# Longer target transfers, earlier statistics and a recut tail in a normalised squared-error loss

## The chip, the cores and the metric

One core of a Trainium2 chip. The time is device microseconds of one execution; lower is better. The profiler's span is some 1.7 us shorter than the reported time (75.1 to 76.86 for the kernel before). Times inside an execution count from the start of that span.

## The reference, cut to what matters

```python
# pred, target: [32, 147, 768] float32
mean = target.mean(axis=-1, keepdims=True)
var = target.var(axis=-1, keepdims=True)
target = (target - mean) / np.sqrt(var + 1e-6)
loss = np.mean((pred - target) ** 2, axis=-1)
return loss.mean(axis=-1)                      # [32]
```

Each of 4704 rows of 768 is normalised by its own mean and variance and compared with its prediction. The 28.9 MB of input are read once; the output is 32 numbers.

## The kernel before

The rows are laid out as 36 columns of 128 rows, 0 to 35, and a rest of 96 rows. A column's way: target and pred are loaded by DMA (all but the first pieces cast to bf16 on the way, issued by GpSimd); VectorE makes the target's statistics; ScalarE takes the root; VectorE the reciprocal; GpSimd normalises into `s`. Then pred minus s is squared and summed in one of three ways: TensorE forms -s + pred in PSUM with two products by identity matrices and ScalarE squares it ("ACT"); VectorE subtracts and ScalarE squares ("DVE+ACT"); or VectorE does both ("DVE"). Below, the "subtraction of 34" is TensorE's product that puts -s of column 34 into PSUM, the "product of 34" the one that adds its pred, and "square 34" ScalarE's square of the result. Towards the end each column, or pair of columns, is split between the first and the last way. The order on each engine is worked out beforehand by a small scheduler from estimated durations, a rank and an earliest time for each operation.

```python
piece("p", 0, 4)
piece("t", 16, 20)          # four columns a transfer
piece("t", 20, 24)
piece("p", 4, 8)
piece("t", 24, 28)
piece("t", 28, 32)
piece("p", 8, 12)
piece("t", 32, 36)
# ... pred in fours to 23, twos to 31, ones to 34, and 35 in two halves
piece("p", KM - 1, KM, 0, half)
piece("p", KM - 1, KM, half, D)
# ...
units = [((c, c + 1), 0, D, "ACT" if c < 14 else "DVE+ACT") for c in range(0, 24, 2)]
# ...
for u in [(c, c + 1) for c in range(26, KM - 4, 2)] + [(c,) for c in range(KM - 4, KM - 1)]:
    m = BANK if u[0] < KM - 2 else half
    units += [(u, 0, m, "ACT"), (u, m, D, "DVE")]
units += [((KM - 1,), 0, half, "ACT"), ((KM - 1,), half, D, "DVE")]
# ... the tail's PSUM tiles, two banks each whatever they hold
pools["parts"] = ctx.enter_context(tc.tile_pool(name="parts", bufs=3, space=bass.MemoryType.PSUM))
zs[u, d0] = pools["parts"].tile([P, 2 * BANK], F32, name="zp")
```

KM is 36, D 768, half 384, BANK 512 (the fp32 columns of one PSUM bank).

Of the kernel before, what the change touches and what calls it, by code (L numbers as in the profile page):

```python
# [7 lines left out]
F32 = mybir.dt.float32  # L8
BF16 = mybir.dt.bfloat16
ALU = mybir.AluOpType  # L10
# [4 lines left out]
def kernel(  # L15
# [9 lines left out]
    B, N, D = pred.shape  # L25
    eps = 1e-6
    P = 128
    J = P // B
    KJ = (N + J - 1) // J
    KM = N - (J - 1) * KJ  # L30
    assert KJ == KM + 1
    RP = B * (J - 1)
    half = D // 2
    BANK = 512
    REST = KM
# [4 lines left out]
    def rows_of(c):  # L40
        return RP if c == REST else P
# [12 lines left out]
    def piece(kind, c0, c1, d0=0, d1=D, q="sw"):  # L54
        stream.append((kind, c0, c1, d0, d1, q))
# [5 lines left out]
    piece("p", REST, REST + 1)  # L61
    piece("t", 12, 16)
    piece("p", 0, 4)
    piece("t", 16, 20)
    piece("t", 20, 24)
    piece("p", 4, 8)
    piece("t", 24, 28)
    piece("t", 28, 32)
    piece("p", 8, 12)
    piece("t", 32, 36)  # L70
    for c in range(12, 24, 4):
# [2 lines left out]
        piece("p", c, c + 2)  # L74
    for c in range(32, 35):
        piece("p", c, c + 1)
    piece("p", KM - 1, KM, 0, half)
    piece("p", KM - 1, KM, half, D)


    groups = [(0, 1), (2, 3), (REST,)] + [tuple(range(c, c + 4)) for c in range(4, KM, 4)]


    units = [((c, c + 1), 0, D, "ACT" if c < 14 else "DVE+ACT") for c in range(0, 24, 2)]
    units.insert(2, ((REST,), 0, D, "ACT"))
    units += [((24,), 0, D, "DVE"), ((25,), 0, D, "DVE+ACT")]
    for u in [(c, c + 1) for c in range(26, KM - 4, 2)] + [(c,) for c in range(KM - 4, KM - 1)]:
        m = BANK if u[0] < KM - 2 else half
        units += [(u, 0, m, "ACT"), (u, m, D, "DVE")]
    units += [((KM - 1,), 0, half, "ACT"), ((KM - 1,), half, D, "DVE")]  # L90



# [3 lines left out]
    def op(name, engine, dur, needs, fn, rank=0.0, early=0.0):  # L97
        by_name[name] = len(ops)
        ops.append((name, engine, dur, needs, fn, rank, early))
# [17 lines left out]
    for i, (kind, c0, c1, d0, d1, q) in enumerate(stream):  # L117
        w = (c1 - c0) * (d1 - d0)
        clock += w * rows_of(c0) / P * 0.915 / D + (0.0 if w >= 4 * D else 0.04)
        lanes[q].append(clock + 1.1)  # L120
        for c in range(c0, c1):
            land[kind, c, d0] = clock + 1.1
        k = len(lanes[q])
        op(("load", i), {"hw": "SP", "hw2": "ACT", "sw": "POOL"}[q], 0.6, [], lambda a=stream[i]: load(*a), rank=-1.0,
           early=0.0 if k <= 8 else lanes[q][k - 9] + 0.3)

    def landed(kind, c):
        return max(t for (k, cc, d), t in land.items() if k == kind and cc == c)

    ident = singles.tile([P, P], BF16)  # L130
# [25 lines left out]
    def bn(out, parts):  # L156

        n = parts[0].shape[0]
        st = small.tile([P, len(parts), 6], F32, name="st")
        for j, x in enumerate(parts):  # L160
            pin(nc.vector.bn_stats(out=st[:n, j, :], in_=x))  # L161
        pin(nc.vector.bn_aggr(out=out, in_=st[:n, :len(parts)]))  # L162

    def stats(g, i):
        n, K = rows_of(g[0]), len(g)
        if i == 0:
            mvs[g] = small.tile([P, K, 2], F32, name="mv")
        if not norm_pix_loss:
            return
        (_, _, til, o), = tbuf[g[i]]  # L170
        bn(mvs[g][:n, i], [til[:n, o + a:o + a + half] for a in (0, half)])

    def root(g):
        n, K = rows_of(g[0]), len(g)
        r = small.tile([P, K], F32, name="r")
        nm = small.tile([P, K], F32, name="nm")
        for i, c in enumerate(g):
            rs[c] = (r[:n, i:i + 1], nm[:n, i:i + 1])
        rs[g] = r
        if not norm_pix_loss:  # L180
            pin(nc.vector.memset(r, 1.0))
            pin(nc.vector.memset(nm, 0.0))
            return
        mv = mvs[g]
        pin(nc.scalar.activation(out=r[:n], in_=mv[:n, :, 1], func=ACTF.Sqrt, bias=eps_t[:n], scale=1.0))  # L185
        pin(nc.scalar.activation(out=nm[:n], in_=mv[:n, :, 0], func=ACTF.Copy, scale=-1.0))  # L186

    def recip(g):
        n = rows_of(g[0])
        if norm_pix_loss:  # L190
            pin(nc.vector.reciprocal(out=rs[g][:n], in_=rs[g][:n]))  # L191

    for k, g in enumerate(groups):
        for i, c in enumerate(g):
            op(("bn", c), "DVE", 1.26, [], lambda g=g, i=i: stats(g, i), rank=k - 50.0 if c < 32 or c == REST else -1.5, early=landed("t", c))
        op(("root", k), "ACT", 0.55, [("bn", c) for c in g], lambda g=g: root(g), rank=-1.0)
        op(("recip", k), "DVE", 0.2, [("root", k)], lambda g=g: recip(g), rank=-60.0)

# [16 lines left out]
    zs = {}  # L215
# [5 lines left out]
    def product(u, d0, w, src, so, eye, first):  # L221
        n, z = rows_of(u[0]), zs[u, d0]

        runs = [(0, so, w)] if w % D == 0 else [(k * BANK, so + k * D, w // len(u)) for k in range(len(u))]
        for zo, o, e in runs:
            for a in range(0, e, BANK):
                b = min(e, a + BANK)
                pin(nc.tensor.matmul(z[:n, zo + a:zo + b], eye[:n, :n], src[:n, o + a:o + b],  # L228
                                     start=first, stop=not first))

    def sub_target(u, d0, w):
        if u in pairs_pe:
            zs[u, d0] = pools["pairs"].tile([P, 3 * BANK], F32, name="z")
            pairs_pe.remove(u)
        else:
            if "parts" not in pools:

                pools["stack"].close()
                pools["parts"] = ctx.enter_context(tc.tile_pool(name="parts", bufs=3, space=bass.MemoryType.PSUM))
            zs[u, d0] = pools["parts"].tile([P, 2 * BANK], F32, name="zp")  # L240
        s, so = sbuf[u[0]]
        product(u, d0, w, s, so + d0, nident, True)

# [30 lines left out]
    rl = singles.tile([P, n_early], F32)  # L274
    rl_sum = singles.tile([P, 1], F32)
    pairs_pe = [u for u, d0, d1, eng in units if eng == "ACT" and (u[0] == REST or len(u) * (d1 - d0) > 2 * BANK)]
    n_pairs = len(pairs_pe)
    pools = {"stack": ExitStack()}
    pools["pairs"] = pools["stack"].enter_context(tc.tile_pool(name="psum", bufs=2, space=bass.MemoryType.PSUM))
    finals = []  # L280
    early_ops, users, dusers, dprev, seen = [], [], [], [], set()
    for k, (u, d0, d1, eng) in enumerate(units):
        w = len(u) * (d1 - d0)
        arrive = max(t for (kk, c, d), t in land.items() if kk == "p" and c in u and d < d1)
        norms = [("norm", c) for c in u]
        for c in u:
            if c not in seen:
                op(("norm", c), "POOL", 1.02, [("recip", group_of[c])], lambda u=u, c=c: normalise(u, c), rank=k)
                seen.add(c)
        if k < len(units) - tail:  # L290
            if u[0] == REST:
                dest = singles.tile([P, 1], F32, name="rl_rest")
                finals.append((("sq", k), dest, mask_rest, RP))
            else:
                dest = rl[:, len(early_ops):len(early_ops) + 1]
                early_ops.append(("sq", k))
        else:
            dest = singles.tile([P, 1], F32, name=f"rl{k}")
            finals.append((("sq", k), dest, mask, P))
        if eng in ("DVE", "DVE+ACT"):  # L300
            op(("diff", k), "DVE", 0.57 * w / D + 0.05, norms + dusers[-5:-4] + dprev[-1:], lambda u=u, d0=d0, w=w: difference(u, d0, w), rank=-2.0,
               early=arrive)
            dusers.append(("sq", k))
            dprev.append(("diff", k))
            if eng == "DVE":
                op(("sq", k), "DVE", 1.0 * w / D, [("diff", k)],
                   lambda u=u, d0=d0, w=w, dest=dest: square_dve(u, d0, w, dest), rank=-1.0)
            else:
                op(("sq", k), "ACT", 0.65 * w / D + 0.22, [("diff", k)],
                   lambda u=u, d0=d0, w=w, dest=dest: square_act(u, d0, w, dest), rank=k)  # L310
            continue
        op(("subt", k), "PE", 0.37 * w / D, norms + (users[-2:-1] if len(users) < n_pairs else users[n_pairs - 1:n_pairs] + users[n_pairs:][-3:-2]) + ["ident"],
           lambda u=u, d0=d0, w=w: sub_target(u, d0, w), rank=k + 0.0)
        op(("pred", k), "PE", 0.37 * w / D, [("subt", k)], lambda u=u, d0=d0, w=w: add_pred(u, d0, w), rank=k,
           early=arrive)
        op(("sq", k), "ACT", 0.65 * w / D + 0.22, [("pred", k)],
           lambda u=u, d0=d0, w=w, dest=dest: square_act(u, d0, w, dest), rank=k)
        users.append(("sq", k))

    acc = psum1.tile([1, B], F32)  # L320
    op("rl_sum", "DVE", 0.2, early_ops, lambda: pin(nc.vector.tensor_reduce(
        out=rl_sum, in_=rl, axis=mybir.AxisListType.X, op=ALU.add)), rank=-3.0)
    finals.insert(0, ("rl_sum", rl_sum, mask, P))
    turn = []

# [5 lines left out]
    for i, (need, vec, m, n) in enumerate(finals):  # L331
        op(("final", i), "PE", 0.2, [need, "masks"], lambda v=vec, m=m, n=n: final(v, m, n), rank=90.0,
           early=max(land.values()) + 0.4)
# [6 lines left out]
    while left:  # L340
        best = None
        for i in left:
            name, engine, dur, needs, fn, rank, early = ops[i]
            if any(x not in end for x in needs):
                continue
            t = max([free[engine], early] + [end[x] + (0.0 if ops[by_name[x]][1] == engine else HOP) for x in needs])
# [4 lines left out]
        _, i, t = best  # L351
        name, engine, dur, needs, fn, rank, early = ops[i]
# [43 lines left out]
```

## Time and profile before

| | before |
|---|---|
| time, median of the first 3 runs | 76.86 us (76.75 to 76.93) |
| span | 75.1 us |
| busy share: PE, DVE, ACT, POOL | 39%, 75%, 40%, 71% |
| DMA share of the software queue | 89% |
| last landing (the last of its 16 completion records) | 71.59 us |
| end of the last sum | 72.65 us (VectorE) |

Read it from the DMA row: only the stream of transfers is busy throughout, so the time is the stream plus what has to follow the last landing. The second part is 72.65 - 71.59 = 1.06 us up to the last sum. The row for the clock that TensorE was granted, in tenths of full speed for 40 slices of 1.88 us:

```profile
PEclk9999999999999999999999755599555797555995
```

It falls to half in stretches, one of which ends at 69.6 us, just before the tail.

### The profile page before, as it was taken

What the parts mean: (1) busy time and instruction counts of PE and PEld (TensorE: products, weight loads), DVE (VectorE), ACT (ScalarE), POOL (GpSimd) and SP (SyncE); (2) the same over time, 40 slices, a digit from 0 to 9 for tenths busy, and PEclk for the clock granted to TensorE, in tenths of its full rate; (3) what the DMA queues carried; (4) which work ended last, traced back from release to release, by engine and by line L of the source; (5) the groups of instructions that cost most, each with busy time, mean ns of one, the idle gap of its engine ahead of it and who ended that gap; (6) DMA issues with size and microseconds to landing.
All of it is one profiled execution on the core that took longest, in us unless ns stands there. A gap on an engine that the chain in (4) does not pass through costs nothing.

```text
span 75.1 us, 551 instructions
## 1 busy us (share of the span) xinstructions
PE 29.0 (39%) x81; PEld 8.3 (11%) x82; DVE 56.3 (75%) x155; ACT 30.4 (40%) x65; POOL 53.7 (71%) x75
## 2 busy tenths in 40 slices
PE   0000000385004989405973006740709300379760
PEld 0000000011001233002121002110103000112130
DVE  0000399999999999999959999375797389998870
ACT  5100001400202696020690010890099969965950
POOL 6998103999499989398989898987695999900000
PEclk9999999999999999999999755599555797555995
DMA  0799999999999999999999999999999999999900
GB/s 0 196 425 317 234 265 218 193 226 213 219 222 209 219 217 209 209 216 213 209 226 219 220 209 219 209 209 213 213 209 232 196 212 214 213 204 208 148 0 0
DMA packets 3685, 15.41 MB, mean 205 GB/s; under 512 B 418, under 2 KB 1154, under 8 KB 3554
## 3 DMA queue, kind: packets, MB, share of 16 engines
q0 software_dynamic: 3424, 13.52, 89.0%
q1 hardware_dynamic: 258, 1.87, 6.9%
q14 instruction: 3, 0.02, 0.1%
HBM read 28.90 MB, written 0.00 MB: 385 GB/s over the span
## 4 chain that ended last, share of the span: by engine, by line
DMA 51%; POOL 32%; issue 7%; DVE 3%; ACT 2%; PE 2%; POOLq 0%
DMA p<-in_pred_dram 29%; POOL s L211 25%; DMA t<-in_target_dram 22%; POOL p L111 4%; ACT zp L249 2%; POOL t L111 2%; DVE zd L269 2%; PE zp L228 1%; DVE zd L265 1%; POOL ident L139 0%; POOL nident L139 0%; PE acc L328 0%; DVE ob L359 0%; POOL nident L138 0%; POOL ident L138 0%
## 5 line engine op out<-in xcount | busy, mean ns | idle before, releaser
L161 DVE BATCH_NORM_STATS2 st<-t 128x6 f32<-128x384 bf16 (+2 forms) x74 | 36.2, 530 | 10.4 <-DMA t<-in_target_dram 10.4
L211 POOL TENSOR_SCALAR s<-t,nm,r 128x768 bf16<-128x768 bf16 (+2 forms) x37 | 38.3, 1043 | 6.2 <-DVE r L191 5.5
L228 PE MATMUL z<-p,ident 128*128 128x512 bf16 (+2 forms) x23 | 10.4, 614 | 18.3 <-DMA p<-in_pred_dram 18.3
L228 PE MATMUL z<-s,nident 128*128 128x512 bf16 (+2 forms) x23 | 9.8, 546 | 16.2 <-POOL s L211 14.9
L249 ACT ACTIVATE z<-z 128x1536 f32<-128x1536 f32 (+1 forms) x8 | 10.9, 1357 | 11.6 <-PE z L228 11.6
L185 ACT ACTIVATE r<-mv,eps_t 128x4 f32<-128x4 f32 (+2 forms) x11 | 3.2, 292 | 27.4 <-DVE mv L162 26.6
L265 DVE TENSOR_TENSOR zd<-p,s 128x1536 bf16<-128x1536 bf16 (+4 forms) x14 | 9.6, 701 | 3.6 <-DMA p<-in_pred_dram 3.5
L111 POOL DMA_DIRECT2D p<-in_pred_dram x16 | 9.1, 570 | 3.5 <-DMA t<-in_target_dram 1.3
L162 DVE BATCH_NORM_AGGREGATE mv<-st 128x2 f32<-128x12 f32 (+1 forms) x37 | 7.7, 208 | 1.3
L249 ACT ACTIVATE zd<-zd 128x1536 bf16<-128x1536 bf16 (+1 forms) x6 | 8.2, 1364 | 0.7 <-DVE zd L265 0.7
L228 PEld LDWEIGHTS <-ident 128*128 128x128 bf16 (+1 forms) x33 | 4.4, 134 | 33.4 <-issue 33.1
L228 PE MATMUL zp<-p,ident 128*128 128x512 bf16 (+1 forms) x9 | 4.3, 519 | 6.9 <-DMA p<-in_pred_dram 6.9
L228 PEld LDWEIGHTS <-nident 128*128 128x128 bf16 (+1 forms) x33 | 3.5, 122 | 29.7 <-issue 16.6
L249 ACT ACTIVATE zp<-zp 128x1024 f32<-128x1024 f32 (+2 forms) x7 | 5.1, 735 | 1.5 <-PE zp L228 1.4
L111 POOL DMA_DIRECT2D t<-in_target_dram x8 | 4.7, 612 | 1.1 <-DMA t<-in_target_dram 1.1
L228 PE MATMUL zp<-s,nident 128*128 128x512 bf16 (+1 forms) x10 | 4.7, 571 | 2.1 <-ACT z L249 1.7
L269 DVE SCALAR_TENSOR_TENSOR zd<-zd 128x512 bf16<-128x512 bf16 (+3 forms) x8 | 5.0, 623 | 0.2
L186 ACT ACTIVATE nm<-mv 128x4 f32<-128x4 f32 (+2 forms) x11 | 2.1, 189 | 0.0
L185 ACT ACT_TABLE_LOAD x1 | 1.3, 1283 | 0.8 <-PEq L377 0.8
L249 ACT ACTIVATION_READ_ACCUMULATOR z<-z 128x1 f32 (+1 forms) x8 | 1.5, 190 | 0.0
L191 DVE RECIPROCAL r<-r 128x4 f32<-128x4 f32 (+2 forms) x11 | 1.4, 128 | 0.1
L249 ACT ACTIVATION_READ_ACCUMULATOR zp<-zp 128x1 f32 x7 | 1.3, 188 | 0.0
(25 smaller groups left out, 7.0 us busy)
## 6 DMA issues: line engine op xcount, KB each, us to landing
t<-in_target_dram POOLq DMA_DIRECT2D x8, 768.0 KB, 23.7
p<-in_pred_dram POOLq DMA_DIRECT2D x6, 768.0 KB, 29.0
t<-in_target_dram SPq DMA_DIRECT2D x1, 1536.0 KB, 8.0
p<-in_pred_dram POOLq DMA_DIRECT2D x4, 384.0 KB, 24.5
p<-in_pred_dram POOLq DMA_DIRECT2D x3, 192.0 KB, 16.4
t<-in_target_dram SPq DMA_DIRECT2D x1, 288.0 KB, 10.6
p<-in_pred_dram POOLq DMA_DIRECT2D x2, 96.0 KB, 9.5
p<-in_pred_dram POOLq DMA_DIRECT2D x1, 144.0 KB, 13.2
```

The costliest lines, as they stand in the source:

```text
L111: pin(eng.dma_start(out=til[:n], in_=src))
L161: pin(nc.vector.bn_stats(out=st[:n, j, :], in_=x))
L162: pin(nc.vector.bn_aggr(out=out, in_=st[:n, :len(parts)]))
L185: pin(nc.scalar.activation(out=r[:n], in_=mv[:n, :, 1], func=ACTF.Sqrt, bias=eps_t[:n], scale=1.0))
L186: pin(nc.scalar.activation(out=nm[:n], in_=mv[:n, :, 0], func=ACTF.Copy, scale=-1.0))
L191: pin(nc.vector.reciprocal(out=rs[g][:n], in_=rs[g][:n]))
L211: pin(nc.gpsimd.tensor_scalar(out=s[:n, so:so + D], in0=til[:n, o:o + D], scalar1=nm, scalar2=r, op0=ALU.add, op1=ALU.mult))
L228: pin(nc.tensor.matmul(z[:n, zo + a:zo + b], eye[:n, :n], src[:n, o + a:o + b], start=first, stop=not first))
L249: pin(nc.scalar.activation(out=z[:n, :w], in_=z[:n, :w], func=ACTF.Square, accum_out=dest[:n]))
L265: pin(nc.vector.tensor_tensor(out=x, in0=y, in1=v, op=ALU.subtract))
L269: pin(nc.vector.scalar_tensor_tensor(out=z, in0=z, scalar=1.0, in1=z, op0=ALU.mult, op1=ALU.mult, accum_out=dest))
```

## The change

Its intent: two transfers fewer; no subtraction of VectorE in front of a statistic, so that the last normalisations aren't late; one pair (14, 15) taken off VectorE; a last part with less for VectorE; and PSUM tiles of the size that is used, so that more of the tail's first products (by s) are made ahead of pred. The diff, comments and unchanged lines cut:

```diff
-    piece("t", 16, 20)
-    piece("t", 20, 24)
+    piece("t", 16, 24)
     piece("p", 4, 8)
-    piece("t", 24, 28)
-    piece("t", 28, 32)
+    piece("t", 24, 32)
 ...
-    piece("p", KM - 1, KM, 0, half)
-    piece("p", KM - 1, KM, half, D)
+    piece("p", KM - 1, KM, 0, BANK)
+    piece("p", KM - 1, KM, BANK, D)
 ...
-    units = [((c, c + 1), 0, D, "ACT" if c < 14 else "DVE+ACT") for c in range(0, 24, 2)]
+    units = [((c, c + 1), 0, D, "ACT" if c < 16 else "DVE+ACT") for c in range(0, 24, 2)]
 ...
-        m = BANK if u[0] < KM - 2 else half
-        units += [(u, 0, m, "ACT"), (u, m, D, "DVE")]
-    units += [((KM - 1,), 0, half, "ACT"), ((KM - 1,), half, D, "DVE")]
+        units += [(u, 0, BANK, "ACT"), (u, BANK, D, "DVE")]
+    units += [((KM - 1,), 0, BANK, "ACT"), ((KM - 1,), BANK, D, "DVE")]
 ...
-            op(("bn", c), ... rank=k - 50.0 if c < 32 or c == REST else -1.5, ...)
+            op(("bn", c), ... rank=k - 50.0 if c < 36 or c == REST else -1.5, ...)
 ...
-                pools["parts"] = ... bufs=3 ...
-            zs[u, d0] = pools["parts"].tile([P, 2 * BANK], F32, name="zp")
+                pools["parts"] = ... bufs=2 ...
+                pools["last"] = ... bufs=3 ...
+            if len(u) == 2:
+                zs[u, d0] = pools["parts"].tile([P, 2 * BANK], F32, name="zp")
+            else:
+                zs[u, d0] = pools["last"].tile([P, BANK], F32, name="zl")
 ...
-    op("rl_sum", ... rank=-3.0)
+    op("rl_sum", ... rank=3.0)
```

More of the change, by code (lines that the diff above doesn't have):

```diff
@@ L194 @@
         for i, c in enumerate(g):
-            op(("bn", c), "DVE", 1.26, [], lambda g=g, i=i: stats(g, i), rank=k - 50.0 if c < 32 or c == REST else -1.5, early=landed("t", c))
+            op(("bn", c), "DVE", 1.26, [], lambda g=g, i=i: stats(g, i), rank=k - 50.0 if c < 36 or c == REST else -1.5, early=landed("t", c))
         op(("root", k), "ACT", 0.55, [("bn", c) for c in g], lambda g=g: root(g), rank=-1.0)
@@ L238, in sub_target @@
                 pools["stack"].close()
-                pools["parts"] = ctx.enter_context(tc.tile_pool(name="parts", bufs=3, space=bass.MemoryType.PSUM))
-            zs[u, d0] = pools["parts"].tile([P, 2 * BANK], F32, name="zp")
+                pools["parts"] = ctx.enter_context(tc.tile_pool(name="parts", bufs=2, space=bass.MemoryType.PSUM))
+                pools["last"] = ctx.enter_context(tc.tile_pool(name="last", bufs=3, space=bass.MemoryType.PSUM))
+            if len(u) == 2:
+                zs[u, d0] = pools["parts"].tile([P, 2 * BANK], F32, name="zp")
+            else:
+                zs[u, d0] = pools["last"].tile([P, BANK], F32, name="zl")
         s, so = sbuf[u[0]]
@@ L280 @@
     finals = []
-    early_ops, users, dusers, dprev, seen = [], [], [], [], set()
+    early_ops, users, dusers, dprev, pusers, lusers, seen = [], [], [], [], [], [], set()
     for k, (u, d0, d1, eng) in enumerate(units):
@@ L311 @@
             continue
-        op(("subt", k), "PE", 0.37 * w / D, norms + (users[-2:-1] if len(users) < n_pairs else users[n_pairs - 1:n_pairs] + users[n_pairs:][-3:-2]) + ["ident"],
+        op(("subt", k), "PE", 0.37 * w / D, norms + (users[-2:-1] if len(users) < n_pairs else users[n_pairs - 1:n_pairs] + (pusers[-2:-1] if len(u) == 2 else lusers[-3:-2])) + ["ident"],
            lambda u=u, d0=d0, w=w: sub_target(u, d0, w), rank=k + 0.0)
@@ L318 @@
         users.append(("sq", k))
+        if len(users) > n_pairs:
+            (pusers if len(u) == 2 else lusers).append(("sq", k))
     acc = psum1.tile([1, B], F32)
     op("rl_sum", "DVE", 0.2, early_ops, lambda: pin(nc.vector.tensor_reduce(
-        out=rl_sum, in_=rl, axis=mybir.AxisListType.X, op=ALU.add)), rank=-3.0)
+        out=rl_sum, in_=rl, axis=mybir.AxisListType.X, op=ALU.add)), rank=3.0)
     finals.insert(0, ("rl_sum", rl_sum, mask, P))
```

## The prediction

> **What bounds the kernel now.** I read the page first, then the chain of waits in order of time, then the timelines of VectorE, TensorE and ScalarE from 49 us on. From the page, the rows for the share of the DMA engines and for what was read:
>
> ```profile
> span 75.1 us, 551 instructions
> ...
> DMA  0799999999999999999999999999999999999900
> ...
> HBM read 28.90 MB, written 0.00 MB: 385 GB/s over the span
> ```
>
> No slice from 3.8 us to 71 us is below nine tenths, while the same page gives VectorE 75% and GpSimd 71%. So the stream of transfers is the bound: 28.9 MB in about 68.5 us is 422 GB/s. The chain of waits names GpSimd for much of the way, but only because GpSimd issues each transfer after one eight places earlier has landed; what decides is its last part:
>
> ```profile
> 45.97 21.79 DMA p<-in_pred_dram
> 67.75 0.04 issue
> 67.79 1.03 PE zp L228 x2
> 68.82 0.02 issue
> 68.84 0.87 ACT zp L249
> 69.71 0.05 issue
> 69.76 0.80 ACT zp L249 x3
> 70.56 0.02 issue
> 70.59 0.05 DVE rl_sum L321
> ...
> 72.07 0.58 DVE zd L269 x2
> 72.65 0.04 issue
> 72.70 0.23 PE acc L328 x2
> 72.93 0.02 issue
> 72.95 0.18 DVE ob L359
> ```
>
> The transfer of pred 30 and 31 was issued at 45.97 and landed at 67.75, so eight queued transfers always hide the issue. After it come the tail's squares, VectorE's last difference and sum (end 72.65), one product (72.93), a copy, the store. From 72.65 to the end of the span is 2.47 us and from span to reported time 1.74 us; neither is touched.
>
> How long a piece occupies the stream is read from what ended waits:
>
> ```profile
> 49.35 1.02 DVE L161 BATCH_NORM_STATS2 st<-t 128x6 f32<-128x384 bf16 x2 [1.72 <-DMA t<-in_target_dram]
> 53.09 0.96 DVE L265 TENSOR_TENSOR zd<-p,s 128x1536 bf16<-128x1536 bf16 x1 [1.28 <-DMA p<-in_pred_dram]
> 56.74 0.96 DVE L265 TENSOR_TENSOR zd<-p,s 128x1536 bf16<-128x1536 bf16 x1 [0.40 <-DMA p<-in_pred_dram]
> 64.07 0.58 PE L228 MATMUL zp<-p,ident 128*128 128x512 bf16 x1 [5.17 <-DMA p<-in_pred_dram]
> 65.92 1.01 PE L228 MATMUL zp<-p,ident 128*128 128x512 bf16 x2 [1.27 <-DMA p<-in_pred_dram]
> 67.79 1.01 PE L228 MATMUL zp<-p,ident 128*128 128x512 bf16 x2 [0.43 <-DMA p<-in_pred_dram]
> ```
>
> Pieces of four columns land 3.65 us apart (53.09 to 56.74), pieces of two 1.86 apart. Two twos cost 3.72, so a piece costs about 0.05 us besides 0.90 us a column. By that rule, from 67.75 the single columns 32, 33, 34 land at 68.70, 69.65, 70.60 and the two halves of 35 at 71.10 and 71.60; the completion records in the trace give 68.69, 69.64, 70.59, 71.10 and 71.59.
>
> **What the Trainium skill says.** "DMA: Bandwidth & Descriptors", section "Anatomy of one DMA — SWDGE (gpsimd) path", gives a transfer as about 2.0 us plus bytes over 436 GB/s, the 2.0 being mostly completion latency. Four columns are 1.573 MB, so 3.61 us by its variable part; the trace has 3.65. The fixed part doesn't show in the spacing since transfers are queued; only about 0.05 us a piece does. "SBUF — State Buffer", section "Who interferes with whom": VectorE with two SBUF inputs and a GpSimd instruction that reads SBUF block each other. The trace agrees: the 128x512 difference at 64.75 took 1.11 us beside a normalisation, those at 66.51 and 67.87, after GpSimd was done, 0.42 and 0.43. "PSUM — Partial Sum Buffer", section "The four PSUM rules": one product writes at most one bank, 512 fp32 columns. Parts before are three tiles of two banks, after it two of two and three of one; with the accumulator's bank 7 and 8 banks, so more buffers fit, and four of seven last parts no longer hold half-empty tiles.
>
> **The change part by part.**
> Pieces of eight: two pieces fewer, 2 x 0.05 = 0.10 us off the stream; all later landings come 0.10 earlier (pred 30 at 67.65, 34 at 70.49, first part of 35 at 71.14, last part at 71.49). The last two parts sum to the same.
>
> What it costs before that: target 16 now lands with 19 to 23. VectorE began column 16 at 28.29; it must now wait until about 31.0 (GpSimd's wait for that transfer ended at 31.3 before). Four columns of statistics with a reciprocal take 4.61 us (28.29 to 32.90), so column 23 is done at 40.2. Target 24 landed at 38.36, so 28 to 31 at 42.0, now 41.9: 1.7 us idle, then eight columns to 51.1 and the last four to 55.8. Before, they ended at 56.34, because VectorE stood still 1.72 at 49.35, then 1.28 in front of the difference of 14 and 15, and did it (0.96) ahead of two columns. That difference now goes to TensorE, and no difference stands ahead of statistics. So the new idle time is paid by the old: a draw. The last roots on ScalarE stand behind the squares of 12 to 15 either way (57.47 before), so the last normalisations don't come earlier.
>
> TensorE: the 12 products for 14 and 15 of about 0.43 us pitch lie in time in which it waited for pred. ScalarE squares that pair either way, at 1.44 us from PSUM instead of 1.47.
>
> The tail, VectorE: two 128x384 units become 128x256. The 384 units ran from 70.69 to 71.68 and from 71.68 to 72.65, about 0.98 each; a 256 unit from 68.95 to 69.70, 0.75. Column 34's is then done at about 71.35, and the last part landed at 71.49 starts at 71.55: end 72.30 against 72.65, 0.35 earlier, now set by landing, not by VectorE. The move of the sum over early columns in rank has no effect: the emitted order keeps it between columns 33 and 34.
>
> The tail, ScalarE: two squares grow from 0.48 to 0.59. Square 30 starts at 68.74 (0.10 earlier), 32 at 69.76. Before, the subtraction of 34 waited for square 30, and the product of 33 behind it came at 70.19, so square 33 began 70.66 though ScalarE was free at 70.56. With one-bank tiles the subtractions of 32, 33, 34 are all made ahead, so square 33 begins at 70.36. But that of 35 takes the buffer of 32, and the order puts it ahead of pred 34: it waits until 0.75 after 69.76 (the distance 69.86 to 70.61 before), 70.51; pred 34 follows at 70.72, its square 0.47 later (70.19 to 70.66 before) at 71.19; square 35 0.59 later at 71.78, and its sum 0.69 later at 72.47. ScalarE before: 72.33. So ScalarE takes VectorE's place at the end. From there two final products instead of one (0.06 us pitch) give 72.81 against 72.93.
>
> The sum: 0.12 us less if the wait of subtraction 35 is as I work it out, 0.35 less if it is hidden. I take about 0.2: 76.65.
>
> **The rivals.**
> First, the tail is all landing: then VectorE's 0.35 is worth the whole, 76.5. For it: VectorE alone is last in the chain. Against: ScalarE ended only 0.32 before it, and its work grows.
> Second, the PSUM wait and the clock make the tail longer. The clock row shows 5 in places (`PEclk 9999...755599555797555995` at its end), and a 512 product had a pitch of 0.43 until 69.5, 0.2 after. With half clock at 70.5, pred 34 comes at 70.94, its square at 71.64, the end of sums 72.92: about 0.3 slower, 77.1. TensorE does 12 more products at about 50 to 55 us, which may shift where the low clock falls. One chance in five.
> Third, the late statistics push through: the subtraction of 34 now stands ahead of pred 26 on TensorE, so a late normalisation would hold up pred 26 (64.07) and its square (65.25). Before, normalisation 34 ran 61.22 to 63.08; GpSimd now has one more normalisation behind the issue of pred 34, so about 63.7. Slack is some 0.3 us. If lost, 77 to 77.5; but squares 28 and 30 wait for landings, so most of such a delay would be absorbed. One in ten.
> Fourth, the 24 KB rows move faster than I count, or longer descriptors are split: the measured 0.05 a piece comes from two against four columns only. Up to 0.3 us more, 76.3.
>
> **Range and chances.** Rivals one and four draw to 76.3 to 76.5, two and three to 77.1; the runs before lie within 0.18 us. So 76.65, eight in ten in 76.3 to 77.0. Two per cent is 1.54 us: neither the stream (0.1) nor the tail (under 0.4) holds that, so faster 0.02, same 0.96, slower 0.02.
>
> **What would show it.** DMA share still nine tenths in every slice; landing of pred 30 0.1 earlier; VectorE idle some 2.7 us at 28.3 and 1.7 at 40.2, none between 51 and 55; last statistics at 55.8; no wait of the product of 33 for a square; a wait of subtraction 35 for square 32 at about 70.5; ScalarE's last sum after VectorE's. Wrong if the landings moved by over 0.3 us, if pred 26 starts later than 64.5, or if the tail's products run at half clock.

## The result, and the profile after

| | before | changed |
|---|---|---|
| median of 6 runs each | 76.83 us (76.75 to 76.93) | 76.66 us (76.48 to 76.91) |
| ratio, 95% interval | | 0.9979 (0.996 to 0.9998) |
| the same again, on chip 1 (e9, below) | 76.91 us | 76.67 us, ratio 0.9971 (0.9953 to 0.999) |

A ratio is the mean time of one kernel's fast runs over that of the other's of the same rounds, so not quite the ratio of the medians. The change is worth about 0.2 us of 77, inside the 2% that count as the same.

From the page of the changed kernel:

```profile
span 74.9 us, 559 instructions
...
PEclk9999999999999999996599985558999555557999
DMA  0899999999999999999998999999999999999800
...
HBM read 28.90 MB, written 0.00 MB: 386 GB/s over the span
```

The stream is as full as it was. VectorE's timeline has the idle time that the pieces of eight were said to bring, and none where the subtraction of 14 and 15 used to stand (the bracket is the idle time just before, and what ended it):

```profile
29.00 0.18 DVE L188 RECIPROCAL r<-r 128x4 f32<-128x4 f32 x1 [1.21 <-ACT r L182]
30.88 1.02 DVE L158 BATCH_NORM_STATS2 st<-t 128x6 f32<-128x384 bf16 x2 [1.71 <-DMA t<-in_target_dram]
...
41.82 1.02 DVE L158 BATCH_NORM_STATS2 st<-t 128x6 f32<-128x384 bf16 x2 [1.73 <-DMA t<-in_target_dram]
...
56.54 0.96 DVE L266 TENSOR_TENSOR zd<-p,s 128x1536 bf16<-128x1536 bf16 x1 [0.89 <-DMA p<-in_pred_dram]
```

Idle for 1.21 + 1.71 us around 29 us and 1.73 at 41.8, then nothing until the landing of pred 16 at 56.5. The last part of the chain of waits, where the prediction shows VectorE for the kernel before, has changed hands, from VectorE to ScalarE:

```profile
66.84 1.77 PE zp L225 x4
...
70.46 0.62 PE zl L225 x2
...
71.11 0.39 ACT zl L250
...
71.79 0.61 ACT zl L250 x2
72.40 0.04 issue
72.45 0.29 PE acc L331 x4
```

The timeline shows the wait in it. First the kernel before, TensorE and ScalarE:

```profile
70.01 0.34 PE L228 MATMUL zp<-s,nident 128*128 128x384 bf16 x1 [0.35 <-ACT zp L249]
70.19 0.38 PE L228 MATMUL zp<-p,ident 128*128 128x512 bf16 x1
...
70.61 0.34 PE L228 MATMUL zp<-s,nident 128*128 128x384 bf16 x1
...
70.66 0.58 ACT L249 ACTIVATE zp<-zp 128x512 f32<-128x512 f32 x1
...
70.78 0.68 PE L228 MATMUL zp<-p,ident 128*128 128x384 bf16 x2
```

and the changed one:

```profile
69.49 0.38 PE L225 MATMUL zl<-p,ident 128*128 128x512 bf16 x1 [0.59 <-DMA p<-in_pred_dram]
...
70.31 0.58 ACT L250 ACTIVATE zl<-zl 128x512 f32<-128x512 f32 x1
...
70.46 0.39 PE L225 MATMUL zl<-s,nident 128*128 128x512 bf16 x1 [0.59 <-ACT zl L250]
...
70.69 0.76 PE L225 MATMUL zl<-p,ident 128*128 128x512 bf16 x2
...
71.11 0.58 ACT L250 ACTIVATE zl<-zl 128x512 f32<-128x512 f32 x1
...
71.69 0.59 ACT L250 ACTIVATE zl<-zl 128x512 f32<-128x512 f32 x1
```

The product of pred 33 no longer waits for a square (69.49, its landing; before 70.19). But the subtraction of 35 waits for square 32 as before (70.46; 70.61 before), and the product of 34 still stands behind it (70.69; 70.78 before). The sums end at 72.40, and VectorE, at 72.24, isn't last any more.

The same chain shows one more wait. There are now two tiles of two banks instead of three, and the subtraction of 30 waits for square 26 (66.84; before, it was made at 57.84). So the product of 30 starts at 67.65, 0.12 us after its landing at 67.53 (before 0.04 after: 67.79 and 67.75), and followed back, the chain meets no landing between the end and that of pred 20 to 23 at 60.16. "Stream plus what follows the last landing" is only a fair approximation for the changed kernel.

The last landing came 0.20 us earlier (71.39 against 71.59); from it to the end of the sums it was 1.01 us, before 1.06. So in this pair of executions nearly all of the gain is in the last landing. How much of that is the change, and how much a stream that happened to begin early, one pair can't tell; the experiments can.

### The profile page after: what moved, and what is told of

The parts are those of the page before. It is cut to its first block, busy times and chain, and to the rows that moved or that the text cites. A ratio compares the mean times of both kernels' runs of the same rounds, so it can differ in the third digit from the quotient of the medians.

```text
span 74.9 us, 559 instructions
## 1 busy us (share of the span) xinstructions
PE 29.1 (39%) x88; PEld 8.5 (11%) x88; DVE 55.1 (74%) x154; ACT 30.8 (41%) x65; POOL 52.9 (71%) x73
## 4 chain that ended last, share of the span: by engine, by line
DMA 59%; ACT 11%; DVE 10%; POOL 9%; issue 4%; PE 4%; ACTq 0%; DVEq 0%; POOLq 0%
DMA p<-in_pred_dram 49%; DMA t<-in_target_dram 10%; POOL s L208 8%; DVE st L158 6%; ACT zd L250 5%; ACT zp L250 3%; PE zp L225 2%; DVE zd L266 2%; ACT zl L250 2%; POOL p L108 1%; DVE mv L159 1%; PE zl L225 1%; PE acc L331 0%; ACT r L182 0%; ACTq L394 0%
## 5 line engine op out<-in xcount | busy, mean ns | idle before, releaser
L250 ACT ACTIVATE z<-z 128x1536 f32<-128x1536 f32 (+1 forms) x9 | 12.3, 1366 | 3.6 <-PE z L225 3.6
L266 DVE TENSOR_TENSOR zd<-p,s 128x1536 bf16<-128x1536 bf16 (+3 forms) x13 | 8.3, 658 | 2.9 <-DMA p<-in_pred_dram 2.9
L250 ACT ACTIVATE zd<-zd 128x1536 bf16<-128x1536 bf16 (+1 forms) x5 | 6.7, 1346 | 1.8 <-DVE zd L266 1.8
L270 DVE SCALAR_TENSOR_TENSOR zd<-zd 128x256 bf16<-128x256 bf16 (+2 forms) x8 | 5.3, 663 | 0.2
L225 PE MATMUL zl<-s,nident 128*128 128x512 bf16 x4 | 2.1, 537 | 5.5 <-POOL s L208 4.9
L250 ACT ACTIVATE zp<-zp 128x1024 f32<-128x1024 f32 x3 | 3.0, 1006 | 0.8 <-PE zp L225 0.8
L225 PE MATMUL zp<-p,ident 128*128 128x512 bf16 x6 | 3.0, 607 | 0.3 <-DMA p<-in_pred_dram 0.3
L225 PE MATMUL zp<-s,nident 128*128 128x512 bf16 x6 | 2.0, 457 | 2.6 <-ACT z L250 2.5
L250 ACT ACTIVATE zl<-zl 128x512 f32<-128x512 f32 x4 | 2.3, 586 | 0.1
L225 PE MATMUL zl<-p,ident 128*128 128x512 bf16 x4 | 1.5, 377 | 0.6 <-DMA p<-in_pred_dram 0.6
```

The costliest lines, as they stand in the source:

```text
L225: pin(nc.tensor.matmul(z[:n, zo + a:zo + b], eye[:n, :n], src[:n, o + a:o + b], start=first, stop=not first))
L250: pin(nc.scalar.activation(out=z[:n, :w], in_=z[:n, :w], func=ACTF.Square, accum_out=dest[:n]))
L266: pin(nc.vector.tensor_tensor(out=x, in0=y, in1=v, op=ALU.subtract))
L270: pin(nc.vector.scalar_tensor_tensor(out=z, in0=z, scalar=1.0, in1=z, op0=ALU.mult, op1=ALU.mult, accum_out=dest))
```

## The experiments

All twelve gave right results. Two measures besides the time:

- **The stream's length, free of its start.** A transfer has sixteen completion records, one from each DMA engine (the Trainium skill, "DMA: Bandwidth & Descriptors", section "Why a DMA increments its semaphore by 16 and not by 1": only all sixteen mean that the data is there). The traces have sixteen for each input transfer. I take the mean of the sixteen times of the last transfer, less the mean for target 12 to 15, the last target transfer before the cuts differ. This isn't last record to last record: that one reads 51.65 in the changed kernel, 51.56 in e1 and 52.07 in e2, and spreads from 51.46 to 51.75 over six kernels whose pieces are the same (changed, e3, e4, e9, e11, e12), so it can't show 0.1 us. The mean lies within 0.02 us over the same six.
- **The tail.** End of the last sum, as the chain of waits has it, less the last landing.

| kernel | median us (range) | ratio to before | stream | last landing | sums end | tail | clock 70 to 71 us |
|---|---|---|---|---|---|---|---|
| before | 76.83 (76.75 to 76.93) | 1 | 51.63 | 71.59 | 72.65 | 1.06 | 1.0 |
| changed | 76.66 (76.48 to 76.91) | 0.9979 | 51.54 | 71.39 | 72.40 | 1.01 | 1.0 |
| e1 fours | 77.37 (76.76 to 77.46) | 1.0045 | 51.64 | 71.57 | 73.03 | 1.46 | 0.5 |
| e2 twos | 77.22 (76.98 to 77.61) | 1.0036 | 51.83 | 71.77 | 73.06 | 1.29 | 1.0 |
| e3 late subtraction | 76.65 (76.48 to 77.21) | 0.998 | 51.54 | 71.40 | 72.27 | 0.87 | 1.0 |
| e4 halves | 76.88 (76.62 to 77.02) | 0.9988 | 51.53 | 71.49 | 72.62 | 1.13 | 0.5 |
| e5 busy | 77.17 (77.04 to 77.50) | 1.0031 | 51.62 | 72.48 | 73.31 | 0.83 | 1.0 |
| e6 busy, fours | 77.24 (77.04 to 77.32) | 1.0028 | 51.70 | 72.15 | 73.03 | 0.88 | 1.0 |
| e7 busy, before | 77.56 (77.24 to 77.63) | 1.0072 | 51.70 | 72.01 | 73.08 | 1.07 | 1.0 |
| e8 busy, late subtraction | 77.17 (77.04 to 77.47) | 1.0031 | 51.61 | 72.03 | 72.87 | 0.84 | 1.0 |
| e9 changed again | 76.67 (76.53 to 76.87) | 0.9971 | 51.55 | 71.42 | 72.50 | 1.08 | 1.0 |
| e10 few busy | 76.79 (76.48 to 77.27) | 0.9998 | 51.55 | 71.52 | 72.56 | 1.04 | 1.0 |
| e11 old statistics | 77.50 (77.12 to 77.86) | 1.0076 | 51.54 | 71.44 | 73.66 | 2.22 | 0.5 |
| e12 two banks | 77.20 (76.68 to 77.47) | 1.0026 | 51.54 | 71.51 | 72.95 | 1.44 | 0.54 |

Times are of six runs each; the columns from "stream" on are of one profiled execution each. e1 to e4 ran on chip 0, e5 to e8 on chip 10, e9 to e11 on chip 1, e12 on chip 9, so times of different groups are best compared by their ratios. By the 2% rule all of these kernels count as the same.

### e1 and e2: pieces of four, pieces of two

```diff
 # e1, against the changed kernel          # e2: all of 16 to 31 in twos
-    piece("t", 16, 24)
+    piece("t", 16, 20)
+    piece("t", 20, 24)
     piece("p", 4, 8)
-    piece("t", 24, 32)
+    piece("t", 24, 28)
+    piece("t", 28, 32)
```

> The changed kernel with target 16 to 31 again in four pieces of four columns; all else as changed. My theory as predicted: each piece costs 0.05 us of the stream, two more pieces make it 0.10 us longer, all later landings come 0.10 later, so about 76.75 us. Rival one: the pieces of eight bought less, since from the landing of target 12 to 15 to the last landing the kernel before took 51.69 us and the changed one 51.65: then 76.66 to 76.70, and that interval reads 51.69 here. Rival two: pieces of eight only bring idle time to VectorE (2.7 us at 28 us, 1.7 us at 40 us) and fours are better: under 76.6.

> Dose: target 16 to 31 in eight pieces of two columns, all else as changed; six pieces more than in the changed kernel. Theory (0.05 us a piece): the interval from the landing of target 12 to 15 to the last landing grows by 0.30 to about 51.95 us, time about 76.95. Rival (a piece costs 0.02 us or less): 51.77 or less and a time within 0.12 of the changed kernel's.

The mean of the stream answers cleanly. With fours it is 51.63 and 51.64; with eights 51.53 to 51.55 in six kernels without useless products, and in e10; with twos 51.83. So two pieces cost 0.09 to 0.10 us and six pieces 0.29: about 0.05 a piece, and the dose has the expected size. (Up to the landing of pred 8 to 11, just behind the recut stretch, the eights save 0.13 or more: 25.57 to 25.59 us against 25.71; some 0.05 of it is given back later, and I don't know by what.) By this measure rival one of e1 is out; rival two is out by the time.

The time of e1 doesn't answer so cleanly: expected 76.75, measured 77.37, with one run at 76.76 and five at 77.31 to 77.46. The profiled execution, one of the five, shows where its 0.6 us lie. Its page, and its timeline:

```profile
PEclk9999999999999999995557965559997555555555
```

```profile
71.07 1.06 PE L227 MATMUL zl<-p,ident 128*128 128x512 bf16 x2
...
71.74 0.58 ACT L252 ACTIVATE zl<-zl 128x512 f32<-128x512 f32 x1 [0.52 <-PE zl L227]
```

TensorE ran at half clock from 58 us to the end. The product of pred 34 comes at 71.07 instead of 70.69 and square 34, after 0.52 us of waiting, at 71.74 instead of 71.11. That is the second rival of the prediction, term by term. That the pieces have little to do with it is argued, not shown; e6 below, at full clock, supports it. The tail is 1.46 us instead of 1.01. In e2's profile the clock was full from 69.9 us on and the tail 1.29: there the chain again meets no landing after pred 20 to 23 (60.92), and the product of 30 starts at 68.19, 0.27 us after its landing. The Trainium skill, "TensorE: Matmul & The Clock Gate", section "Part 1: The HAM clock gate (the "warmup" mystery)", says that the clock is set by TensorE's recent activity in a window that runs freely and doesn't start with the kernel, so that the point of change differs from run to run. The traces agree in that full clock comes back at 68.4 (changed), 69.4 (e3) and 70.9 us (e12), or not before the end (e1, e4), in kernels that do nearly the same work. Of the window they show only that the clock changes at steps of 3.41 us or a multiple (in the kernel before at 49.1, 52.5, 59.3, 62.7, 69.6 and 73.0 us).

The record also has the mean granted clock of each execution. In e1 it is 0.79 to 0.82 in the five slow runs and 0.87 in the fast one; in e3, below, 0.76 and 0.81 in the two slow runs and 0.85 to 0.87 in the four others. In e9 there is no such order: its slowest run, 76.87, has the highest clock, 0.869. So a low clock goes with the runs that are clearly slow; how it makes them slow is seen in one profile, that of e1.

### e3: the subtraction of 35 behind the product of 34

```diff
-           lambda ...: sub_target(u, d0, w), rank=k + 0.0)
+           lambda ...: sub_target(u, d0, w), rank=60.0 if u[0] == KM - 1 else k,
+           early=land["p", KM - 2, 0] + 0.05 if u[0] == KM - 1 else 0.0)
```

> The changed kernel with TensorE's subtraction of column 35 behind the product of pred 34 instead of ahead of it, nothing else moved. Theory (the wait of that subtraction for square 32 makes ScalarE the last engine): square 34 starts at 70.9 instead of 71.1, square 35 at about 71.5, ScalarE's last sum ends about 72.2, and the end is then shared with VectorE at 72.24; 0.15 to 0.2 us faster than the changed kernel, about 76.5. Rival (the landing of the last part and VectorE set the end already): within 0.05 us of the changed kernel.

```profile
70.45 0.38 PE L225 MATMUL zl<-p,ident 128*128 128x512 bf16 x1 [0.56 <-DMA p<-in_pred_dram]
70.66 0.38 PE L225 MATMUL zl<-s,nident 128*128 128x512 bf16 x1
...
70.96 0.58 ACT L250 ACTIVATE zl<-zl 128x512 f32<-128x512 f32 x1
...
71.56 0.58 ACT L250 ACTIVATE zl<-zl 128x512 f32<-128x512 f32 x1
```

The product of 34 comes at its landing (70.45), the subtraction of 35 after it. Squares 34 and 35 start at 70.96 and 71.56 instead of 71.11 and 71.69, with the last landing at 71.40 against 71.39, and the sums end 0.13 us earlier. So the wait of this subtraction does set the end of the changed kernel at full clock. The times don't show it: four runs at 76.48 to 76.67, two at 77.11 and 77.21, median 76.65. The theory holds in the trace; the gain of 0.15 in the time doesn't show.

### e4: the cut of 384 and 384

```diff
-    piece("p", KM - 1, KM, 0, BANK)
-    piece("p", KM - 1, KM, BANK, D)
+    piece("p", KM - 1, KM, 0, half)
+    piece("p", KM - 1, KM, half, D)
 # and the units of 34 and 35 cut at half, as in the kernel before
```

> The changed kernel with columns 34 and 35 cut 384 and 384 again (both the landing pieces of 35 and the units), all else as changed. Theory: VectorE's two last units take 0.98 instead of 0.75 us each, so it ends about 72.5 instead of 72.24, while ScalarE's last sum comes about 0.2 earlier, 72.2: VectorE last again, and about 0.05 to 0.1 us slower than the changed kernel. Rival (the cut is worth nothing because ScalarE gets what VectorE gives): within 0.03 us.

Undecided. The profile fell on half clock (70 to 73 us), where ScalarE and VectorE end together (72.62 and 72.56), not VectorE last as expected. Its tail at half clock, 1.13 us, is 0.33 shorter than that of e1 at half clock with the cut of 512 and 256. Shorter products and squares at the end may be why; e1 differs in its pieces of four too, and the reason isn't tested. The ratio, 0.9988, is between before and the changed kernel and its interval (0.9967 to 1.001) holds both. That the new cut gains anything isn't shown.

### e5 to e8: TensorE kept busy

If the low clock is what spreads the times, work that nobody uses should remove it. After certain products each kernel repeats a product into the accumulator's bank (43 times; in the kernel before 47 by the edit, though its expectation says 46), which the final sums overwrite:

```diff
+    def keep_busy(times, src, so, eye):
+        for _ in range(times):
+            pin(nc.tensor.matmul(spare, eye, src[:, so:so + BANK], start=True, stop=True))
-    acc = psum1.tile([1, B], F32)
+    acc = spare[:1, :B]          # spare: one whole bank
```

> The changed kernel plus 43 products of TensorE that nothing uses (into the accumulator's bank, ahead of the final sums), placed where TensorE waits from 53 us on, so that it is hardly ever idle. Theory (the granted clock in the last 3 us is a matter of chance from run to run, 1.0 or 0.5, and at 0.5 the product of pred 34 and its square come 0.3 to 0.5 us later): the clock row shows no 5 from about 57 us on, the runs lie within 0.2 us of each other, all like the changed kernel's fast ones, 76.5 to 76.7, and none near 76.9 or above. Rival one (the clock follows chance whatever TensorE does): spread as before, 76.5 to 76.9. Rival two (useless products hold up the useful ones): slower, over 76.9, with TensorE ahead of ScalarE in the chain.

> The same useless products in the kernel with target 16 to 31 in four pieces of four (the one that came out at 77.37, with half clock at its end in the profile). Theory (those 0.7 us were the clock of its last microseconds, not the pieces): about 76.65 to 76.75, that is 0.05 to 0.10 above the busy changed kernel. Rival (pieces of four cost 0.5 us or more in this order of statistics): stays near 77.3.

> The kernel before with 46 useless products in the waits of TensorE from 53 us on. Theory (VectorE sets its end, ScalarE 0.3 us behind it, so the clock matters less): about 76.75 to 76.85, its spread of 76.67 to 77.13 shrinks to 0.2 or so; the change is then worth about 0.2 us at equal clock. Rival (the spread of before has nothing to do with the clock): 76.7 to 77.1 as it was.

> The changed kernel with both: useless products, and the subtraction of column 35 behind the product of pred 34. Theory: square 34 starts 0.15 us earlier than in the busy changed kernel at the same landing, ScalarE and VectorE end together near 72.2; 0.1 to 0.15 us faster than the busy changed kernel, about 76.45 to 76.5, and the best of all. Rival (no gain over the busy changed kernel, since landings vary more than that): within 0.05.

All four times missed: 77.17 to 77.56. Yet the clock did what was asked: 1.0 from 60 us at the latest to 75 us in all four profiles, and tails of 0.83 to 0.88 us where ScalarE is last (in e5 and e8 VectorE ends within 0.03 us of it). The spread, though, stayed: 0.46, 0.28, 0.39 and 0.43 us, against 0.43 in the changed kernel, so that the clock makes the spread isn't shown by these four. With full clock the kernel of fours is no longer 0.6 us worse than that of eights (77.24 and 77.17). The gain of the late subtraction that e8 was to show didn't come (77.17 as in e5, tail 0.84 against 0.83): its rival came true. What went wrong is in the stream. The rows of e5's page for its queues, and the landing of pred 28 in its timeline:

```profile
q14 instruction: 3, 0.02, 0.1%
q8 instruction: 1, 0.02, 0.1%
```

```profile
67.16 0.59 PE L225 MATMUL zp<-p,ident 128*128 128x512 bf16 x2 [1.76 <-DMA p<-in_pred_dram]
```

TensorE's records in the trace, weight loads included, had grown from 182 to 266, and a second instruction queue appears with one packet: 16 KB, 0.96 us long, at 65.09 us. Pred 28 landed at 67.12; fifteen of its sixteen records were there by 65.69, as in other kernels, and the sixteenth was 1.43 us late. It stays behind: at the last transfer fifteen engines were done at 71.40, the sixteenth at 72.48. The mean over the engines (51.62) hardly shows it. All four busy kernels have this packet, between 64.1 and 65.4 us; of the others only e10 has it, later (below). That the packet delays one engine is the reading that fits the records of all four, in each of which the sixteenth record falls behind at the next landing or the one after. A smaller case is in e11: a packet of 8 KB on the first instruction queue at 66.86 us, and the sixteenth record of pred 30 comes 0.48 us behind the fifteenth (68.03), but pred 32 is level again. That the packet fetches TensorE's longer list is inferred from the count of records.

### e9 and e10: the changed kernel again, and fewer useless products

e10 is e8 with 14 useless products in place of 43 (210 records of TensorE in the trace; the expectation counts rows in another way).

> The changed kernel as it is, a second time, on the same chip as the next two. Theory: two kinds of runs, those with full clock in the last 3 us at 76.5 to 76.75 and those with half clock there at 76.9 to 77.3; if the profiled run is of the second kind, the product of pred 34 comes at 70.9 and square 34 at 71.5 or later instead of 71.11, with the landings where they were. Rival (the clock plays no part, the spread is that of the landings): the spread follows the landing of the last part and square 34 stands at 71.1.

> The changed kernel with the late subtraction of column 35 and only 14 useless products (182 rows on TensorE instead of 240 in the busy kernel). Theory (what spoiled the busy kernels was one more fetch of instructions, 16 KB in 0.95 us at 65 us on one of the sixteen DMA engines, whose pieces then landed 0.6 to 1.1 us behind the others'): no such packet on a second instruction queue, the last landing back at 71.4, clock 1.0 in the last 3 us in every run, all runs at 76.45 to 76.65, none of the slow kind (two of six of the late subtraction alone were at 77.1 to 77.2): the best version. Rival one (the fetch comes here too): last landing 72 or later, 77.0. Rival two (14 are not enough to hold the clock): slow runs at 77.1 among them, as without.

e9 gave 76.53 to 76.87 and a profile at full clock, from 68.5 us on, with square 34 at 71.20 and the last landing 0.03 us later. Of its two kinds of runs only one was seen, so it supports neither side; with the first six, 11 of 12 executions of the changed kernel lie under 76.9. Its tail, 1.08 us, is that of the kernel before (1.06).

e10's page has the packet too, against its expectation:

```profile
q8 instruction: 1, 0.02, 0.1%
```

But it comes at 72.23 us, 0.7 us after the last landing, which is back at 71.52, and no engine is late. So the delay goes with a packet inside the stream, as far as five kernels can show; 43 products against 14 is the other difference. The 14 products didn't hold the clock: it was 0.5 from 61.9 to 68.7 us, where the useless products held up the product of pred 30 (67.94; 67.65 in the changed kernel). The slow runs of rival two came (77.19 and 77.27), but not in its way: five of the six spans are 74.8 us and one 75.1, and the mean clock of the two slow ones is 0.92 and 0.90. Up to 0.8 us of the time lies outside the profiled span, in no other kernel here; the late packet is the one new thing near the end of the profile, and whether it has to do with this isn't shown. No version is shown to beat the changed kernel.

### e11: the statistics as before, under pieces of eight

```diff
-    ... "ACT" if c < 16 else "DVE+ACT" ...
+    ... "ACT" if c < 14 else "DVE+ACT" ...
-    ... rank=k - 50.0 if c < 36 or c == REST else -1.5 ...
+    ... rank=k - 50.0 if c < 32 or c == REST else -1.5 ...
```

> The changed kernel with the pieces of eight but with the last four columns' statistics ranked behind subtractions and 14 and 15 subtracted by VectorE, both as before. Theory (the statistics part of the change does nothing by itself but pays for the idle time that the pieces of eight bring): three subtractions stand ahead of the last statistics, these end after 58.5 instead of 55.6, the last reciprocal stands behind the subtraction of 20 and 21 (landing 60.2), the last four normalisations run from 61 to 67 or 68, in time for pred 35 at 71 but close; 0.1 to 0.3 us slower, 76.8 to 76.95. Rival one (all that slack is unused): as the changed kernel within 0.05. Rival two (the normalisations come too late and TensorE's subtractions hold up the squares): 77.3 or more.

Expected 76.8 to 76.95, measured 77.5: rival two. GpSimd and ScalarE in its timeline:

```profile
62.88 6.39 POOL L208 TENSOR_SCALAR s<-t,nm,r 128x768 bf16<-128x768 bf16 x4
...
70.08 1.01 ACT L250 ACTIVATE zp<-zp 128x1024 f32<-128x1024 f32 x1 [2.18 <-PE zp L225]
```

The last reciprocal came at 61.09, and the last four normalisations took until 69.27, 1.6 us each in this stretch, where VectorE subtracts and squares nearly all the time. Before the first of them, at 62.88, GpSimd had stood 1.34 us in front of the issue of a transfer that waits for a landing. TensorE's subtraction of 34 waited for one of them and held up pred 30, so that ScalarE stood still for 2.18 us before square 30. The tail is 2.22 us. Part of that is half clock, which this profile has to 72 us; but the best of six runs, 77.12, is still above all 12 of the changed kernel. So this part is worth some 0.8 us once the pieces of eight are there (77.50 against 76.67 of e9, on the same chip). That it moves nothing by itself, under pieces of four, wasn't tested, nor its two halves, the order of the statistics and the pair 14 and 15, apart. I had judged its slack too large.

### e12: tiles of two banks

The changed kernel with the PSUM pool of the kernel before (three tiles of two banks).

> The changed kernel with three tiles of two banks for all last parts, as before, instead of two of two banks and three of one. Theory: the subtractions of 33 and 34 wait again for squares 28 and 30, so the product of 33 comes at about 69.97 instead of 69.49 and square 33 at about 70.44 instead of 70.31; but the subtraction of 35 waits for square 32 at about 70.46 in either kernel and stands ahead of the product of 34, so square 34 stays at about 71.1: within 0.05 us of the changed kernel at full clock in the tail. Rival (the one-bank tiles carry the gain of the change): 0.15 us or more slower than the changed kernel, square 34 at 71.25 or later at full clock.

```profile
70.32 0.63 PE L225 MATMUL zp<-p,ident 128*128 128x512 bf16 x1
...
71.05 0.58 ACT L246 ACTIVATE zp<-zp 128x512 f32<-128x512 f32 x1 [0.58 <-PE zp L225]
```

One run at 76.68, five at 76.98 to 77.47. In the profile, the clock was 0.5 up to 70.9 us. The product of 33 again stands behind a subtraction that waits for a square (69.92), takes 0.63 us at half clock, and square 33 starts at 71.05 instead of 70.31. In e1, at half clock with tiles of one bank, it starts at 70.52: so at half clock the wait by the tiles is real, 0.53 us at this square. What it adds to the end isn't settled, for the tail of 1.44 us is that of e1 (1.46), whose clock stayed at 0.5 for longer; the two delays stand in for one another. By its time the rival's mark, 0.15 us slower than the changed kernel, was met (ratio 1.0026 against 0.9979), but the rival, like the theory, was stated for full clock in the tail, and there it is neither shown nor refuted; the single run at 76.68 goes with the theory. How much of the gain the one-bank tiles carry stays open.

## Why the prediction was right, point by point

**The bound.** Right in the main: the DMA row stays at eight or nine tenths in both kernels from 4 us to 71 us, and the whole of the change is 0.16 us by the first ratio (0.0021 of 76.8) and 0.22 by the second.

**The stream, 0.10 us.** Right, and the best-founded term: 0.09 to 0.10 in the length free of the start, and 0.29 for the six pieces of e2. The two spacings that the prediction names give 0.07 a piece (3.72 less 3.65); its 0.05 fits only with the single columns, 0.95 apart. In the mean of the sixteen records the last transfer of the first pair of profiles came 0.29 us earlier (71.26 and 70.97), and 0.20 of that was there at target 12 to 15 already (19.63 and 19.43), before the first changed piece.

**Statistics a draw.** Right for the whole change: idle 2.9 us near 29 and 1.73 at 41.8 (predicted 2.7 and 1.7), last statistics at about 55.7 (55.8). What the prediction did not say is how much hangs on it. It counted the new idle time against the old and gave the reordering no price; e11 prices it at 0.8 us, with some half clock in it.

**The tail's VectorE.** 72.24 measured, 72.30 predicted, and set by the landing, as said.

**The tail's ScalarE.** The wait of subtraction 35: 70.46 (70.51 predicted), square 34 at 71.11 (71.19), sums at 72.40 (72.47). e3 shows that this wait is the last one. The takeover by ScalarE came as predicted. Not foreseen was that the subtraction of 30 waits for square 26, now that there are two tiles of two banks. And the prediction counts 12 more products for 14 and 15; there are 6 (26 products into `z` each way in the trace instead of 23).

**The sum.** The working gave 0.12 with that wait and 0.35 without it, and I took 0.2. The wait was there, so the working's own answer is 0.12: 0.10 in the stream and next to nothing in the tail. The profiles say the same (tail 1.06 before, 1.01 and 1.08 changed). The two ratios, 0.16 and 0.22, are a little more; both of their intervals hold 0.12. The stated 76.65 is thus closer to the measured 76.66 than the working entitles it to be.

**The rivals.** The first (all landing, 0.35) was ruled out by ScalarE. The second, half clock at the end, is real and its sizes are right (pred 34 at 71.07 against 70.94 predicted, square 34 at 71.74 against 71.64), but it came in other kernels more than in this one. Five of six runs of e1 were slow; of twelve of the changed kernel two are near 76.9 and none above. Whether the changed kernel's order of work brings the clock back earlier (68.4 and 68.5 us in its two profiles) or was lucky is open. The third: the subtraction of 34 did stand ahead of pred 26, and ran at 63.94, so pred 26 came at 64.32 instead of its landing; square 26 (65.67) stood behind ScalarE's own work and lost nothing. e11 shows this rival in full where the normalisations come later still. The fourth is out: eights save what the 0.05 a piece says.

## What to carry to other kernels

In a kernel bound by its transfers, count pieces as well as bytes: here 0.05 us each, measured as the distance between landings in the mean of their sixteen records, which the noise of the start doesn't touch. Look at what stands in front of what in each engine's list, for a step that looks free can be what keeps another one free (e11). Before a few tenths of a microsecond are put down to a change, see which clock the last products had, and whether the trace has new packets, and when: half clock at the end (0.45 us of tail in e1) and one more packet in the stream (1.08 us of one engine in e5) were each worth more than the whole change.

## What the Trainium skill lacked or had wrong

- "DMA: Bandwidth & Descriptors": it prices a transfer's fixed cost at about 2.0 us and explains it as latency, but has no figure for what one more transfer costs in a queue that is never empty: 0.05 us here (stream 51.54, 51.64 and 51.83 us with 2, 4 and 8 pieces for the same bytes).
- "Runtime: NRT & Kernel Launch", section "Instruction fetch mechanics", has instructions fetched in blocks of 16 KiB at a cost that is "mostly hidden", and no page prices this traffic for a stream of data: one 16 KB packet on a second instruction queue took 0.96 us at 65.09 us, after which one of sixteen engines stayed 1.1 us behind the others, and with it every landing (71.40 for fifteen engines, 72.48 for the last).
- "TensorE: Matmul & The Clock Gate": it puts the penalty of the ramp at the start under 1% of a typical span and has no figure for a tail that falls on half clock: 0.45 us in e1 (1.46 against 1.01), twice the effect under study here. Its advice to leave TensorE no idle gaps of over some 3 us kept the clock full in e5, and the time still rose (ratio 1.0031 against 0.9979), with the packet above in the stream.
- No page says why the time outside the profiled span should differ between executions of one kernel: it is 1.66 to 1.78 us in all executions of the other experiments and of the changed kernel, but up to 2.47 in e10.
